# Moving five more stores of a mixture of softmaxes to ScalarE's DMA queue, with a new written order for the last ten units

## The chip, the cores and the metric

The kernel runs on one core of one Trainium2 chip. The metric is the device time of one execution, in microseconds (us), from the first instruction to the last. A profile of one execution lists every instruction and every DMA packet with its time; its span leaves out a little at both ends, so the execution's own time stands beside the span below.

## The reference

The input holds 32 batches of 128 rows, and in each row four heads with 4096 logits each. The output is one row of 4096 values: the four softmaxes, weighted with a softmax over the four prior values of that row.

```python
prior_probs = np.exp(prior - prior.max(axis=-1, keepdims=True))
prior_probs = prior_probs / prior_probs.sum(axis=-1, keepdims=True)
softmax = np.exp(logits - logits.max(axis=-1, keepdims=True))
softmax = softmax / softmax.sum(axis=-1, keepdims=True)
mixture = np.sum(prior_probs[..., None] * softmax, axis=2)   # logits: (32, 128, 4, 4096)
```

Everything is float32. The logits are 268.4 MB to be read, and the output is 67.1 MB to be written.

## The kernel before

**Tiles.** One batch is a *unit* (u = 0 to 31); its 128 rows lie on the 128 partitions. A head of a unit is a tile of 128x4096 floats, 2.1 MB. On-chip memory holds a ring of 12 such slots, thus three units. Head h of unit u goes to slot (4u + h) mod 12 (`place`, L101; the very last head is put one further), so unit u + 3 reuses the slots of unit u.

**Steps.** The kernel has no scheduler: the order is written out by hand as a string of words, and `run` (L193) turns each word into one call. A word names the step, then a head or the quarters of the 4096 columns it covers, then the unit (`@u`; in the repeated part `'` means the unit before and `+2` two units on). The quarters are 1024 columns wide: `34` is the last one, `03` the first three.

- L: load heads (L115, on SyncE's queue SP). `L03@u` brings heads 0 to 2 in one transfer of 6.3 MB, `L34@u` brings head 3.
- M: maximum of a head, negated (VectorE, L123). E: exponential with its sum (ScalarE, L128). R: reciprocal of the sum (VectorE, L134).
- G: a diagonal matrix of the head's weight (GpSimd, L137). X: the head times that diagonal, added up in the PSUM accumulator `acc` (TensorE, L146): `X123` is head 1, quarter 2 to 3. Heads 0 to 2 are summed in this way.
- C: the weight alone (GpSimd, L153). Z: head 3 (or a part of head 2) scaled in place (GpSimd, L157).
- A: head 3 weighted and added to the accumulator (VectorE, L163). For other quarters V copies the accumulator to head 1's slot (ScalarE, L182), and P adds it to the scaled head 3 (GpSimd, L185). W adds a scaled quarter of head 2 to head 3 (GpSimd, L179); for the quarters named in `BYPASS` head 2 is not sent through TensorE. B and T do the like on VectorE for the last unit.
- S: the store of a finished unit (L120). The result lies in head 3's slot, so `S@u` must have landed before `L34@u+3` may be issued.

**What sets the order.** Each engine works through its own instructions in the order of the words and waits by semaphore for its inputs. The two DMA queues (SP's and ScalarE's, q1 and q10 in the profile) each take transfers in the order in which their engine issued them; both are served by the same 16 DMA engines. A DMA instruction whose input isn't ready holds up everything behind it on its engine. Units 0 to 23 repeat one string (`STEADY`, L27): there, `S'` stands between two exponentials, and `L03+2 L34+2` follow. From unit 24 on, `ORDER` (L32 to L59) is a long string in which the steps of two units are mixed, matrix products are cut into quarters, and loads of units 29 to 31 are cut into heads. The queue of a store is chosen by its unit number in `store` (L118): ScalarE's for units 2 to 21, SP's for the others.

Of the kernel before, what the change touches and what calls it, by code (L numbers as in the profile page):

```python
# [26 lines left out]
STEADY = (  # L27
    "M0 E0 R3' C3' Z324' M1 R0 G0 A01' A12' V23' P23' V34' P34' E1 X0 S' L03+2 L34+2 "
    "M2 E2 R1 G1 X1 M3 E3 R2 G2 X2 "
)  # L30
ORDER = [STEADY] * 24
ORDER += [  # L32
    "M1@24 M0@24 E1@24 V23@23 M2@24 E0@24 R3@23 V34@23 R0@24 C3@23 G0@24 A01@23 Z324@23 "
    "X023@24 E2@24 R1@24 A12@23 X001@24 P23@23 M3@24 X012@24 P34@23 X034@24 R2@24 G1@24 "  # L34
    "E3@24 G2@24 X123@24 X112@24 M0@25 X101@24 S@23 X134@24 R3@24 E0@25 X212@24 M1@25 "
    "Z324@24 X234@24 C3@24 L03@26 X223@24 V34@24 A12@24 E1@25 P34@24 X201@24 R0@25 M3@25 "
    "G0@25 X012@25 V23@24 X034@25 P23@24 A01@24 E3@25 X023@25 M2@25 X001@25 R1@25 E2@25 "
    "R3@25 G1@25 C3@25 X134@25 Z324@25 L34@26 M0@26 X123@25 X101@25 S@24 X112@25 R2@25 "
    "E0@26 M1@26 G2@25 X201@25 X234@25 L03@27 X212@25 V34@25 R0@26 M3@26 G0@26 E1@26 "
    "P34@25 X223@25 X034@26 A12@25 V23@25 E3@26 P23@25 M2@26 X013@26 A01@25 E2@26 R1@26 "  # L40
    "X001@26 R3@26 G1@26 Z324@26 X101@26 L34@27 R2@26 G2@26 M0@27 C3@26 X123@26 X112@26 "
    "S@25 X134@26 M1@27 E0@27 X212@26 X234@26 L03@28 R0@27 X201@26 V34@26 M2@27 G0@27 "
    "E1@27 P34@26 X223@26 X034@27 A01@26 V23@26 M3@27 X001@27 E2@27 P23@26 X023@27 R1@27 "
    "E3@27 A12@26 G1@27 X123@27 R2@27 G2@27 Z234@27 X012@27 L34@28 R3@27 Z304@27 X112@27 "
    "M0@28 X212@27 X134@27 V12@27 C3@27 S@26 W34@27 M1@28 E0@28 X223@27 P12@27 X101@27 "
    "X201@27 L01@29 V34@27 R0@28 M2@28 G0@28 E1@28 P34@27 X034@28 X012@28 L12@29 V01@27 "
    "R1@28 M3@28 G1@28 X112@28 E2@28 P01@27 X001@28 X101@28 L23@29 M0@29 V23@27 E3@28 "
    "P23@27 X023@28 X134@28 R2@28 M1@29 Z224@28 L34@29 X123@28 E0@29 G2@28 X202@28 R3@28 "
    "V23@28 R0@29 C3@28 G0@29 S@27 A01@28 Z314@28 E1@29 M2@29 X001@29 X023@29 W23@28 "
    "V12@28 L01@30 V34@28 X012@29 R1@29 P12@28 M3@29 E2@29 X034@29 G1@29 W34@28 X101@29 "  # L50
    "L12@30 E3@29 R2@29 X112@29 P34@28 M0@30 X134@29 G2@29 P23@28 X201@29 V34@29 L23@30 "
    "R3@29 E0@30 M1@30 X123@29 Z304@29 X223@29 L34@30 V01@29 X212@29 C3@29 R0@30 V23@29 "
    "G0@30 M2@30 Z234@29 X001@30 E1@30 P01@29 X023@30 L01@31 W34@29 X034@30 V12@29 R1@30 "
    "M3@30 E2@30 X012@30 G1@30 P12@29 X112@30 L12@31 P34@29 X123@30 E3@30 M0@31 X134@30 "
    "P23@29 X101@30 L23@31 V34@30 R2@30 R3@30 G2@30 M1@31 E0@31 Z314@30 X223@30 X201@30 "
    "C3@30 L34@31 Z234@30 X212@30 V23@30 R0@31 A01@30 G0@31 E1@31 W34@30 X023@31 M2@31 "
    "X001@31 P34@30 S@28 V12@30 X034@31 P23@30 R1@31 E2@31 M3@31 X012@31 G1@31 P12@30 "
    "X134@31 S@29 X123@31 R2@31 E3@31 C2@31 G2@31 B234@31 X101@31 B223@31 S@30 X201@31 "
    "R3@31 C3@31 T23@31 X112@31 T34@31 X212@31 A01@31 S23@31 A12@31 S34@31 S01@31 S12@31 "  # L59
]  # L60

BYPASS = {
    (27, 3), (28, 2), (28, 3), (29, 3), (30, 3), (31, 2), (31, 3),
}


# [1 line left out]
def kernel(  # L68
# [6 lines left out]
    nc = tc.nc  # L75
# [31 lines left out]
    def home(u, a, b):  # L107
        return slot(u, 3, a, b)
# [7 lines left out]
            h += n  # L116

    def store(u, a=0, b=4):  # L118
        queue = nc.scalar if 2 <= u < 22 else nc.sync
        queue.dma_start(out=out[u, :, a * C : b * C], in_=home(u, a, b))  # L120

    def peak(u, h):
# [61 lines left out]
    def add_scaled(u, a, b):  # L184
        nc.gpsimd.tensor_add(home(u, a, b), slot(u, 1, a, b), slot(u, 3, a, b))  # L185

    step = {
        "L": load, "S": store, "M": peak, "E": exp, "R": recip, "G": diagonal, "X": weigh,
        "C": weight, "Z": scale, "A": add_last, "B": add_head, "T": add_both, "V": evac,
        "P": add_scaled, "W": add_second,  # L190
    }

    def run(u, words):  # L193
        for w in words.split():
            op, digits, back, on, at = re.fullmatch(
                r"([A-Z])(\d*)('*)(?:\+(\d+))?(?:@(\d+))?", w
            ).groups()
            v = int(at) if at else u - len(back) + int(on or 0)
            if 0 <= v < U:
                step[op](v, *map(int, digits))  # L200

    with tc.manual_schedule():
# [22 lines left out]

        for u, words in enumerate(ORDER):
            run(u, words)
# [30 lines left out]
```

## Time and profile before

| | |
|---|---|
| three runs | 787.1, 787.2, 787.32 us (median 787.2) |
| the profiled execution | 787.09 us, span 785.4 us |
| TensorE busy | 681.8 us, 87% of the span |
| VectorE busy | 645.1 us, 82% |
| ScalarE busy | 547.5 us, 70% |
| GpSimd busy | 293.8 us, 37% |
| DMA | 335.90 MB at a mean of 428 GB/s |
| packets of q1 (SP) and q10 (ScalarE) | 87.1% and 12.5% of 16 engines' span |

The row of DMA in the profile's picture of 40 slices says how busy the 16 DMA engines were; the rows of the engines say the same for each engine. A share of 100% for DMA means that packets lay end to end on all 16. In the list of waits, "SPq L115 <- DMA out_dram<-ring" is SP standing at a load until a store has landed. Such a wait is harmless as long as earlier transfers are still queued; how long they last is read from the time between the issue of a transfer and its first packet.

### The profile page before, as it was taken

How to read it: one execution, taken by the hardware profiler on the slowest of the kernel's cores; microseconds unless marked ns; L12 is line 12 of the kernel's file. 1: busy time of each engine (PE TensorE's matmuls, PEld its weight loads, DVE VectorE, ACT ScalarE, POOL GpSimd, SP SyncE). 2: the span in 40 equal slices, each digit the busy share in tenths (PEclk: the TensorE clock that was granted, in tenths of full speed). 3: DMA queues.
4: the chain of work that ended last, by engine and by line, in shares of the span. 5: the costliest groups of instructions: out<-in, count | busy, mean ns of one | idle time of the engine just before them, and what ended most of it. 6: DMA issues, size and time to landing. Idle time of an engine off the chain costs nothing.

```text
span 785.4 us, 4589 instructions
## 1 busy us (share of the span) xinstructions
PE 681.8 (87%) x1508; PEld 293.0 (37%) x1508; DVE 645.1 (82%) x327; ACT 547.5 (70%) x326; POOL 293.8 (37%) x243
## 2 busy tenths in 40 slices
PE   0959998989999888998989989898888998899996
PEld 0424433333344333433334334343333443344342
DVE  6489977897778977779877798777888887979895
ACT  2557867867668666686676776766857668779883
POOL 0033323433134332334322343323430544277892
PEclk9989999999989999999999989999989899999999
DMA  9999999999999999999999999999999999999998
GB/s 378 456 411 426 429 436 413 433 437 441 435 416 431 448 436 421 434 424 436 444 429 430 420 436 438 439 427 421 432 449 421 440 408 431 451 412 431 429 429 351
DMA packets 15335, 335.90 MB, mean 428 GB/s; under 512 B 1712, under 2 KB 1712, under 8 KB 2256
## 3 DMA queue, kind: packets, MB, share of 16 engines
q1 hardware_dynamic: 12384, 293.61, 87.1%
q10 hardware_dynamic: 2928, 42.01, 12.5%
q8 instruction: 12, 0.20, 0.1%
q14 instruction: 11, 0.09, 0.0%
HBM read 268.50 MB, written 67.11 MB: 427 GB/s over the span
## 4 chain that ended last, share of the span: by engine, by line
DMA 58%; DVE 12%; PE 10%; POOL 10%; ACT 5%; issue 4%; SPq 0%; POOLq 0%; ACTq 0%
DMA ring<-in_logits_dram 58%; DVE nmax L123 11%; PE acc L146 10%; POOL ring L185 7%; ACT ring L128 3%; ACT ring L182 2%; POOL ring L179 1%; POOL ring L157 1%; POOL diag L137 1%; DVE ring L163 0%; SPq L115 0%; DVE rden L134 0%; SPq L120 0%; POOLq L185 0%; POOLq L137 0%
## 5 line engine op out<-in xcount | busy, mean ns | idle before, releaser
L146 PE MATMUL acc<-ring,diag 128*128 128x512 f32 x1508 | 681.8, 613 | 96.6 <-ACT ring L182 62.0
L123 DVE TENSOR_REDUCE nmax<-ring 128x1 f32<-128x4096 f32 x128 | 563.0, 4409 | 114.6 <-DMA ring<-in_logits_dram 114.6
L128 ACT ACTIVATE ring<-ring,nmax 128x4096 f32<-128x4096 f32 x128 | 474.6, 3708 | 202.5 <-DVE nmax L123 202.1
L146 PEld LDWEIGHTS acc<-ring,diag 128*128 128x128 f32 x1508 | 293.0, 196 | 484.5 <-issue 358.2
L185 POOL TENSOR_TENSOR ring<-ring 128x1024 f32<-128x1024 f32 x68 | 160.1, 2374 | 20.1 <-ACT ring L182 11.2
L137 POOL TENSOR_SCALAR diag<-ident,rden,pp 128x128 f32<-128x128 f32 x96 | 43.0, 448 | 239.7 <-DVE rden L134 239.7
L153 POOL TENSOR_TENSOR wght<-rden,pp 128x1 f32<-128x1 f32 x33 | 6.3, 190 | 210.4 <-DVE rden L134 210.4
L182 ACT ACTIVATE ring<-acc 128x1024 f32<-128x1024 f32 x68 | 66.7, 1012 | 17.9 <-PE acc L146 13.8
L157 POOL TENSOR_SCALAR ring<-ring,rden,pp 128x2048 f32<-128x2048 f32 (+3 forms) x35 | 74.2, 2121 | 9.0 <-DVE rden L134 8.7
L163 DVE SCALAR_TENSOR_TENSOR ring<-ring,wght,acc 128x1024 f32<-128x1024 f32 x60 | 74.2, 1269 | 3.3 <-PE acc L146 2.3
L134 DVE RECIPROCAL rden<-dsum 128x1 f32<-128x1 f32 x128 | 19.3, 153 | 10.2 <-ACT ring L128 10.2
L128 ACT ACTIVATION_READ_ACCUMULATOR ring<-ring,nmax 128x1 f32 x128 | 24.2, 189 | 0.0
L179 POOL TENSOR_TENSOR ring<-ring 128x1024 f32<-128x1024 f32 x5 | 11.8, 2367 | 0.1
L213 DVE TENSOR_REDUCE pmax<-pr 32x128 f32<-32x512 f32 x1 | 0.7, 674 | 5.3 <-DMA pr<-in_prior_dram 5.3
L215 ACT ACTIVATE pr<-pr 32x512 f32<-32x512 f32 x1 | 0.6, 628 | 4.2 <-DVE pr L214 4.2
L163 DVE SCALAR_TENSOR_TENSOR ring<-ring,wght 128x1024 f32<-128x1024 f32 x2 | 2.5, 1280 | 0.3 <-POOL wght L153 0.3
L215 ACT ACT_TABLE_LOAD x1 | 1.3, 1283 | 1.2 <-PEq L242 1.2
L222 DVE STREAM_TRANSPOSE pp<-pn 32x128 f32<-32x128 f32 x4 | 1.2, 302 | 0.1
L216 DVE TENSOR_REDUCE pmax<-pr 32x128 f32<-32x512 f32 x1 | 0.7, 674 | 0.7 <-ACT pr L215 0.7
L218 DVE TENSOR_TENSOR pn<-pr,pmax 32x512 f32<-32x512 f32 x1 | 1.0, 1016 | 0.0
L217 DVE RECIPROCAL pmax<-pmax 32x128 f32<-32x128 f32 x1 | 0.9, 941 | 0.0
L214 DVE TENSOR_TENSOR pr<-pr,pmax 32x512 f32<-32x512 f32 x1 | 0.7, 680 | 0.0
(6 smaller groups left out, 0.9 us busy)
## 6 DMA issues: line engine op xcount, KB each, us to landing
ring<-in_logits_dram SPq DMA_DIRECT2D x27, 6144.0 KB, 34.3
ring<-in_logits_dram SPq DMA_DIRECT2D x43, 2048.0 KB, 25.5
out_dram<-ring ACTq DMA_DIRECT2D x20, 2048.0 KB, 16.1
out_dram<-ring SPq DMA_DIRECT2D x11, 2048.0 KB, 14.0
out_dram<-ring SPq DMA_DIRECT2D x4, 512.0 KB, 5.5
pr<-in_prior_dram ACTq DMA_DIRECT2D x1, 64.0 KB, 4.5
ring<-in_logits_dram SPq DMA_DIRECT2D x1, 39.5
```

The costliest lines, as they stand in the source:

```text
L123: nc.vector.tensor_reduce(out=nmax[:, u, h : h + 1], in_=slot(u, h), op=ALU.max, axis=AX.X, negate=True)
L128: nc.scalar.activation(slot(u, h), slot(u, h), AF.Exp, bias=nmax[:, u, h : h + 1], accum_out=dsum[:, u, h : h + 1],)
L134: nc.vector.reciprocal(rden[:, u, h : h + 1], dsum[:, u, h : h + 1])
L137: nc.gpsimd.tensor_scalar(out=diag[:, u % 2, h], in0=ident, scalar1=rden[:, u, h : h + 1], scalar2=pp[:, h, u : u + 1], op0=ALU.mult, op1= ...
L146: nc.tensor.matmul(acc[:, k * W : (k + 1) * W], lhsT=diag[:, u % 2, h], rhs=e[:, k * W : (k + 1) * W], start=h == 0, stop=h == H - 2 or (u ...
L153: nc.gpsimd.tensor_mul(wght[:, u, h : h + 1], rden[:, u, h : h + 1], pp[:, h, u : u + 1])
L157: nc.gpsimd.tensor_scalar(out=e, in0=e, scalar1=rden[:, u, h : h + 1], scalar2=pp[:, h, u : u + 1], op0=ALU.mult, op1=ALU.mult,)
L163: nc.vector.scalar_tensor_tensor(out=o, in0=slot(u, h, a, b), scalar=wght[:, u, h : h + 1], in1=more, op0=ALU.mult, op1=ALU.add,)
L179: nc.gpsimd.tensor_add(e, e, slot(u, 2, a, b))
L182: nc.scalar.activation(slot(u, 1, a, b), acc[:, a * C : b * C], AF.Copy)
L185: nc.gpsimd.tensor_add(home(u, a, b), slot(u, 1, a, b), slot(u, 3, a, b))
L215: nc.scalar.activation(pr, pr, AF.Exp)
```

## The change

The stores of units 22 to 26 are issued by ScalarE instead of SP. The repeated string ends two units earlier (22 copies instead of 24), and the written order from unit 22 on is a new one. The set of quarters that bypass TensorE changes from seven to eight: units 27, 28 (2), 29, 30 and 31 (2) become units 25, 28, 29 (2), 30 (2) and 31 (2). All other functions stay the same. The diff, cut to the lines of the new order from the store of unit 24 on, and to the same places of the old one:

```diff
-ORDER = [STEADY] * 24
+ORDER = [STEADY] * 22
 ORDER += [
...
-    "P23@27 X023@28 X134@28 R2@28 M1@29 Z224@28 L34@29 X123@28 E0@29 G2@28 X202@28 R3@28 "
-    "V23@28 R0@29 C3@28 G0@29 S@27 A01@28 Z314@28 E1@29 M2@29 X001@29 X023@29 W23@28 "
-    "V12@28 L01@30 V34@28 X012@29 R1@29 P12@28 M3@29 E2@29 X034@29 G1@29 W34@28 X101@29 "
...
-    "P23@29 X101@30 L23@31 V34@30 R2@30 R3@30 G2@30 M1@31 E0@31 Z314@30 X223@30 X201@30 "
-    "C3@30 L34@31 Z234@30 X212@30 V23@30 R0@31 A01@30 G0@31 E1@31 W34@30 X023@31 M2@31 "
-    "X001@31 P34@30 S@28 V12@30 X034@31 P23@30 R1@31 E2@31 M3@31 X012@31 G1@31 P12@30 "
-    "X134@31 S@29 X123@31 R2@31 E3@31 C2@31 G2@31 B234@31 X101@31 B223@31 S@30 X201@31 "
-    "R3@31 C3@31 T23@31 X112@31 T34@31 X212@31 A01@31 S23@31 A12@31 S34@31 S01@31 S12@31 "
...
+    "G1@25 X101@25 L03@27 S@24 M0@26 E2@25 X112@25 X034@25 X134@25 R2@25 E0@26 R3@25 "
+    "G2@25 M1@26 Z234@25 X123@25 C3@25 Z324@25 X201@25 V34@25 W34@25 X223@25 R0@26 E1@26 "
+    "M2@26 X212@25 G0@26 P34@25 X034@26 V23@25 L34@27 A12@25 E2@26 P23@25 X023@26 R1@26 "
+    "M3@26 X012@26 G1@26 X123@26 L03@28 X112@26 R2@26 E3@26 M0@27 G2@26 X212@26 X134@26 "
+    "V12@26 A01@25 E0@27 X223@26 R3@26 M1@27 C3@26 Z314@26 X001@26 X101@26 V23@26 P12@26 "
+    "S@25 X234@26 R0@27 E1@27 M3@27 G0@27 X201@26 P23@26 X012@27 V34@26 A01@26 X023@27 "
+    "E3@27 P34@26 R1@27 M2@27 X001@27 G1@27 X123@27 S@26 X112@27 R3@27 E2@27 M0@28 C3@27 "
+    "Z304@27 X034@27 L34@28 X134@27 R2@27 E0@28 M1@28 G2@27 X101@27 L01@29 X213@27 V12@27 "
...
+    "L34@29 X123@28 R2@28 M1@29 G2@28 E0@29 Z234@28 X201@28 X223@28 L01@30 V34@27 R3@28 "
+    "X212@28 R0@29 Z324@28 M2@29 V23@28 X034@28 E1@29 P34@27 X134@28 C3@28 G0@29 A01@28 "
+    "P23@28 X023@29 V34@28 S@27 M3@29 E2@29 X001@29 W34@28 X034@29 P34@28 A12@28 E3@29 "
+    "L12@30 R1@29 X012@29 R2@29 M0@30 G1@29 Z224@29 X101@29 G2@29 X201@29 L23@30 R3@29 "
...
+    "G2@30 Z224@30 X112@30 L23@31 X123@30 V34@30 R3@30 E0@31 Z314@30 X101@30 M1@31 "
+    "X212@30 L34@31 W34@30 X201@30 V12@30 R0@31 V23@30 M2@31 G0@31 P12@30 X034@31 E1@31 "
+    "S@29 X012@31 W23@30 X023@31 E2@31 R1@31 M3@31 G1@31 C3@30 X134@31 P34@30 S@28 "
+    "X123@31 P23@30 A01@30 E3@31 X112@31 R2@31 C2@31 X001@31 G2@31 B223@31 S@30 B234@31 "
+    "X101@31 R3@31 C3@31 T34@31 X201@31 T23@31 X212@31 A01@31 S34@31 A12@31 S23@31 S01@31 "
+    "S12@31 "
 ]
 BYPASS = {
-    (27, 3), (28, 2), (28, 3), (29, 3), (30, 3), (31, 2), (31, 3),
+    (25, 3), (28, 3), (29, 2), (29, 3), (30, 2), (30, 3), (31, 2), (31, 3),
 }
 
     def store(u, a=0, b=4):
-        queue = nc.scalar if 2 <= u < 22 else nc.sync
+        queue = nc.scalar if 2 <= u < 27 else nc.sync
         queue.dma_start(out=out[u, :, a * C : b * C], in_=home(u, a, b))
```

In each engine's own order, the new one differs from the old at these places. On ScalarE the stores stand like this: `E2@23 S@22 E3@23`, `E3@24 S@23 E2@24`, `E3@25 S@24 E2@25`, then `E0@27 V23@26 S@25 E1@27 V34@26 E3@27 S@26 E2@27`. On SP no store stands among the loads of units 25 to 29; `S@27` comes behind `L01@30` and ahead of `L12@30`, and `S@29` ahead of `S@28`. On GpSimd `P34@27` comes behind `Z234@28` and `Z324@28`. On TensorE one quarter of one head is four instructions in the profile, and one quarter more bypasses it, so there are 1504 of them instead of 1508.

## The prediction

> **What bounds the kernel now.** I read the head of the page first (span, DMA row), then the windows by stage, then the DMA issues and SP's waits, and last the chain of waits at the end.
>
> ```profile
> DMA  9999999999999999999999999999999999999998
> q1 hardware_dynamic: 12384, 293.61, 87.1%
> q10 hardware_dynamic: 2928, 42.01, 12.5%
> out_dram<-ring ACTq DMA_DIRECT2D x20, 2048.0 KB, 16.1
> out_dram<-ring SPq DMA_DIRECT2D x11, 2048.0 KB, 14.0
> ```
>
> The DMA engines are busy in every slice, and the two queues' packets together fill 99.6% of 16 engines' span. A store lands 16.1 us after its issue on ScalarE's queue and 14.0 us after on SP's. By stages (columns: window, busy time and instructions of each engine, TensorE's clock, DMA share, GB/s):
>
> ```profile
> 97.00:582.00 485.00, 431.32 (x958) 185.87 (x956) 398.11 (x199) 338.39 (x200) 163.28 (x141) 0.96 1.00 432
> 582.00:703.00 121.00, 110.97 (x241) 47.52 (x242) 102.29 (x51) 87.14 (x52) 50.38 (x39) 0.94 1.00 428
> 703.00:776.00 73.00, 69.71 (x159) 29.37 (x159) 66.75 (x35) 64.96 (x42) 57.35 (x39) 1.00 1.01 429
> 776.00:785.30 9.30, 2.36 (x6) 0.76 (x4) 2.75 (x3) 0.00 (x0) 0.00 (x0) 0.89 0.67 273
> ```
>
> With stores on ScalarE's queue (97 to 582) the share is 1.00 at 432 GB/s; with stores on SP's (582 to 703) it is 1.00 at 428. Only the last 9 us fall off. So DMA bounds the time up to about 776 us, and the end of the compute chain bounds the rest. In the stage that is changed, SP does wait, mostly for stores to land:
>
> ```profile
> SPq L115 <- DMA out_dram<-ring: 78.0, 6, 17.1
> SPq L120 <- DVE ring L163: 53.1, 10, 9.8
> SPq L120 <- POOL ring L185: 39.3, 5, 17.9
> ```
>
> The reader should see that these waits, from 580 us on, cost nothing yet: the share in the same window is 1.00. How near they come is in the trace's packet records, put to transfers in the order of their queue: in the stage from 586 us a transfer's first packet comes 3.3 us (the store issued at 617.10) to 19.9 us after its issue, mostly 6 to 12 us. That is the backlog which covers a wait. At the end:
>
> ```profile
> 755.08 3.38 DVE nmax L123
> 758.46 0.91 ACT ring L182
> ...
> 767.79 10.58 PE acc L146 x24
> 778.37 0.03 issue
> 778.39 1.28 DVE ring L163
> ```
>
> The chain runs over the maximum of the last unit's head 1, GpSimd, and TensorE's last 24 products to the last addition; the last store follows it.
>
> **The change part by part.** The sum is made against the profiled execution: 787.09 us, its span 785.4 and 1.7 around it. The median of the runs is 787.2, 0.1 above. What a measurement can tell from no change I take as 0.2%, 1.57 us.
>
> *Bytes and issue time.* Nothing is added to the 335.90 MB. Five issues move from SP (0.34 us each in the rows of its timeline) to ScalarE (0.36). That is 1.8 us on an engine that is 70% busy, beside exponentials; in the repeated stage twenty of these lie there at a DMA share of 1.00. Cost 0. If DMA were not the cover, an exponential would come 0.36 us later.
>
> *The store's wait on ScalarE.* Behind it stands one exponential. With T for the landing of a unit's three-head load (M starts 0.99 us later: 133.46 to 134.45), maxima of 4.41 and exponentials of 3.7, `S@22` to `S@24` come behind an exponential that ends 18 to 21 us after T. Their last inputs P take two or three GpSimd steps (2.05 + 2.37 + 2.37) after a reciprocal at T + 10, so T + 17. No stall; 0. SP in turn runs ahead: `L03@26` to `L03@28` go out at about T + 17 with some 11 us queued.
>
> *The slower rate of 582 to 703.* By the windows it is worth 121 us x (1 - 428/432) = 1.1 us at most. By the packets it is less: the 16 KB packets of the stage take 611 to 614 ns in most transfers, 621 and 651 in two, and all that they lie above 611 (and the 48 KB ones above 1815) sums to 0.6 us, in a patch at 622 to 645 us that no store order explains. Ends 0 and -1.1; I take -0.3, near the packets.
>
> *`L34@28`, the thin place.* `S@25` stands on ScalarE behind `E0@27`: T27 + 0.99 + 4.43 + 3.9, and V's 0.9, thus issued at T27 + 10.3. In before it went at 662.98, that is T27 - 3.9 (T27 was 666.90), and the load that needs its slot at 677.02, with 11.0 us still queued. Now the store's first packet comes 3.4 us after issue (100.14 to 103.50 in the repeated stage), at T27 + 13.7. Beside the three-head load, each engine takes a 48 KB packet and a 16 KB one in turn: the repeated stage's store took 103.50 to 115.31 for eight packets per engine, which alone need 8 x 0.611 = 4.9 us. So `L34@27`, `L03@28` and `S@25` (4.9 + 14.5 + 4.9) are through together at T27 + 24.3, with the store the last. `L34@28` goes out 1.0 us after (115.31 to 116.29) and starts 0.9 to 2.0 us after that (the issues at 775.15 and 770.09 found a short queue). On SP's queue nothing else may pass it, so 1.9 to 3.0 us stand open. What fills them is `S@26`, queued behind `S@25`: M0, one addition of 1.27, M1 and M3 end at T27 + 15.8, `E3@27` at T27 + 19.6; issued at 19.8, first packet at 23.2, covered till 29.2. It is 1.1 us in time. Ends 0 and +3.0; I take 0, because each step has a row, and the cover is 2 to 3 us long.
>
> The Trainium skill says otherwise of sharing: in "DMA: Bandwidth & Descriptors", "Queues, rings and completion order", each engine takes turns between queues by whole packets of some 9 to 17 descriptors. By that, a store's eight pieces would go in one turn, `S@25` would be through at about T27 + 19, an estimate, and the place would not be thin at all. The 11.8 us of the trace's stores speak against it, and the sum keeps to them.
>
> *`S@27` and the loads behind it.* The store is issued by SP and holds up `L12@30`, `L23@30`, `L34@30`. Its input `P34@27` now stands behind `Z324@28`, which needs a reciprocal that VectorE gave at 717.7 in before. 717.9 + 2.05 + 2.37 and issue make 722.4, perhaps 2 us less since `L03@28` lands earlier. In before it went at 712.36 with 5.9 us queued. The queue now holds `L01@30` ahead of it, to 718.84 + 4.9 = 723.7; with 0.9 to 2.0 us to the first packet, 0 to 0.7 us stand open. I take +0.2. GpSimd is the one behind; `Z224@29` and later steps have slack, for its steps from `G1@29` to `W34@30` sum to some 27 us of 40.
>
> *The end.* `G0@31` waits for GpSimd:
>
> ```profile
> 755.29 2.91 POOL L157 TENSOR_SCALAR ring<-ring,rden,pp 128x3072 f32<-128x3072 f32 x1
> 758.18 0.18 POOL L153 TENSOR_TENSOR wght<-rden,pp 128x1 f32<-128x1 f32 x1
> 758.35 1.19 POOL L157 TENSOR_SCALAR ring<-ring,rden,pp 128x1024 f32<-128x1024 f32 x1
> 759.74 0.45 POOL L137 TENSOR_SCALAR diag<-ident,rden,pp 128x128 f32<-128x128 f32 x1 [0.21 <-DVE rden L134]
> ```
>
> Ahead of it there is now `Z314@30`, free to start at 754.8, and `W34@30`: 754.8 + 2.91 + 2.37 = 760.1, against 759.74. Both orders have ten quarters (40 products) behind it, 18.2 us in before, so TensorE ends 0.4 us later, and with it the last addition and the last store. `S@30` goes at about 770.9 (before 770.09), as the stores ahead of it end at 772.6: 0.3 us open, but not on the last store's path. The quarter more that bypasses TensorE (4 products of about 0.44) lies earlier. Cost +0.4. Ends: -0.9 (what of the 2 us of idle DMA before 783.96 a better order could get) and +0.9.
>
> Sum: 0 + 0 - 0.3 + 0 + 0.2 + 0.4 = +0.3. On the median: 787.2 + 0.3 = 787.5.
>
> **The rivals.**
>
> *Slower: the cover of `L34@28` fails.* If `S@26` is issued after T27 + 20.9, DMA runs dry. All later loads wait for `L34@28` and go out that much later. Its price is at most 3.0 us, typically 2.4: 787.5 + 2.4 = 789.9. For it: the backlog falls from 11.0 us to none on q1, and the margin is one short step of ScalarE. Against it: ScalarE is idle 30%. From 1.3 us of dry time on (0.3 are there already) it decides the sign.
>
> *Slower: `P34@27` is later than reckoned.* One more GpSimd step of 2.37 us ahead of it, or `V34@27` late behind `E0@29`, opens 0.7 to 2.4 us at `S@27`: up to 789.6, typically 788.6. For it: a step moved back by 10 us (712.36 to 722.4). Against: VectorE's row is dense there, and its order the same.
>
> *Faster: the loads gain.* SP is freed of five waits, the slow patch goes (-0.6 to -1.1), and the end gains up to 0.9: 787.2 - 0.6 - 0.6 = 786.0 typically, 785.2 with all. For it: 432 against 428 GB/s. Against: the share is 1.00 on both sides, so there is no gap to close; faster needs both gains nearly whole.
>
> The Trainium skill speaks against this gain: "DMA: Bandwidth & Descriptors", "Issuing engines are not separate DMA queues", says that DMAs of both queues run on the same 16 engines, and several issuers save only issue time. The trace agrees in the packets, 611 and 1815 ns in either stage.
>
> That the change doesn't do what it says can't be: q10 must rise by five stores of 2.1 MB.
>
> **How the numbers follow.** Forecast (786.8 to 788.4 on its own): 0.61. The cover fails: 0.15. `P34@27` late: 0.10, half of it over the bound. Gain: 0.14, of which 0.06 lies below 785.6. Slower by over 0.2% is 0.15 + 0.05 and 0.01 of the forecast's own spread, 0.21; faster 0.06; same 0.73. The range goes from 786.2 (half of the gain cut off) to 789.7 (most of the cover's case within, with its longest gaps cut off).
>
> **What would show it.** In the changed profile: q10 at about 15.6% (12.5 + 5 x 0.6), q1 at 84; SP's waits for a store's landing without a dip in GB/s. The window of 24 us after T28 shows the cover: a share of 1.00 says it holds; 0.9 or less in 2 us says that it fails. `S@25` issues 10 us after T27, `S@26` 9.5 us after that; `S@27` near 721 to 722. The share at 722 to 726 shows the second rival. At the end, `G0@31` near 760.1 and the last addition near 778.7. The prediction is wrong if a load is issued later than its queue lasts at a place I have not walked (units 22 to 24), or if TensorE's clock, 0.86 to 1.00 by window, slows the new order of products.

## The result, and the profile after

The changed kernel takes 788.46 us (median of 18 executions), the kernel before 787.09 us beside it (18 executions). The ratio of the means is 1.0022 (of the medians 1.0017), with a 95% interval of 1.0015 to 1.0029: slower by about 0.2%. A second session gave 789.65 against 787.39, ratio 1.0026 (1.0017 to 1.0035). More telling than the median is the scatter: executions of the kernel before lie between 786.52 and 787.80 us, those of the changed one between 786.86 and 791.18. The profile that came with the result is of the shortest one, 786.86 us (span 785.1), which is even 0.2 us shorter than the profiled execution of before.

The page of that execution, DMA row, queues and stores (the line numbers of the changed kernel are 7 higher: its loads are L122, its products L153, its copies L189):

```profile
DMA  9999999999999999999999999999999999999998
q1 hardware_dynamic: 11664, 283.12, 84.0%
q10 hardware_dynamic: 3648, 52.50, 15.6%
out_dram<-ring ACTq DMA_DIRECT2D x25, 2048.0 KB, 16.1
out_dram<-ring SPq DMA_DIRECT2D x6, 2048.0 KB, 12.7
```

Its windows by stage (the columns as before: window, busy time of each engine, clock, DMA share, GB/s) and SP's waits from 580 us on:

```profile
97.00:582.00 485.00, 432.45 (x957) 185.91 (x956) 399.52 (x200) 339.01 (x200) 163.23 (x140) 0.96 1.00 432
582.00:703.00 121.00, 107.60 (x243) 45.30 (x242) 101.38 (x50) 88.80 (x55) 51.90 (x39) 0.99 1.00 429
703.00:776.00 73.00, 69.73 (x160) 29.53 (x159) 67.98 (x38) 62.49 (x39) 56.11 (x38) 1.00 1.01 429
```

```profile
SPq L122 <- DMA out_dram<-ring: 92.9, 6, 31.3
```

The five stores moved, and this execution is no slower for it. But SP's longest wait for a store to land grew from 17.1 to 31.3 us. That is the wait of `L34@28` for `S@25`, and it ends with nothing queued: the load goes out at 691.09, its first packet comes 0.97 us later, at 692.06.

So the question is what a longer execution does. One of 790.07 us is among the runs below, with every word of the program the same. Three windows of the short one and then of the long one; the clock is the third number from the end:

```profile
625.00:640.00 15.00, 15.00 (x36) 6.59 (x35) 14.66 (x8) 12.39 (x9) 7.76 (x6) 1.00 1.01 432
657.00:666.00 9.00, 9.00 (x21) 4.09 (x22) 5.08 (x4) 7.49 (x5) 3.25 (x3) 1.00 0.98 421
666.00:688.00 22.00, 18.82 (x44) 8.01 (x43) 20.04 (x10) 15.29 (x10) 12.11 (x9) 1.00 1.00 431
```

```profile
625.00:640.00 15.00, 14.27 (x27) 6.16 (x28) 13.73 (x9) 11.43 (x7) 7.16 (x6) 0.80 1.01 433
657.00:666.00 9.00, 9.00 (x22) 3.99 (x21) 4.89 (x4) 7.25 (x4) 3.10 (x3) 1.00 0.84 343
666.00:688.00 22.00, 18.90 (x38) 7.92 (x37) 19.37 (x9) 14.25 (x9) 11.00 (x7) 0.84 1.00 415
```

From 625 to 640 us the granted clock of TensorE was 0.80 instead of 1.00; from 657 to 666, 17 us later, DMA moved 343 GB/s instead of 421. (In windows as short as these the share itself is off by up to 0.06, since packets that cross an edge are counted on one side; therefore idle DMA is given below from the packets, as the time in which fewer than 16 lay open, each missing one counted as a sixteenth.) The chain of waits of the long execution joins the two:

```profile
625.23 0.46 POOL diag L144
625.69 0.04 issue
625.73 11.45 PE acc L153 x20
637.18 0.02 issue
637.20 0.04 ACT ring L189
...
640.71 23.12 DMA out_dram<-ring
...
664.36 27.63 DMA ring<-in_logits_dram
```

The reader should see a chain that the chain of before never had: TensorE's products of unit 24, ScalarE's copy of them (L189), a store (`S@24`, issued at 640.71 after GpSimd's addition), 23 us until it has landed, and only then the loads behind. In the short execution the second copy of unit 24 starts at 633.58 and `S@24` goes out at 637.94; in the long one at 637.20 and 640.71, 2.77 us later. Not all of that is the clock: 1.04 us were there already at the first maximum of unit 25, which waits for `L03@25` to land and starts at 619.53 in the short and at 620.57 in the long execution.

```profile
633.58 1.02 ACT L189 ACTIVATE ring<-acc 128x1024 f32<-128x1024 f32 x1 [0.50 <-PE acc L153]
```

```profile
637.20 1.02 ACT L189 ACTIVATE ring<-acc 128x1024 f32<-128x1024 f32 x1 [2.35 <-PE acc L153]
```

### The profile page after: what moved, and what is told of

Read it like the earlier page. It is cut to its first block, busy times and chain, and to the rows that moved or that the text cites. A ratio compares the mean times of both kernels' runs of the same rounds, so it can differ in the third digit from the quotient of the medians.

```text
span 785.1 us, 4581 instructions
## 1 busy us (share of the span) xinstructions
PE 679.1 (86%) x1504; PEld 290.8 (37%) x1504; DVE 646.2 (82%) x328; ACT 547.0 (70%) x325; POOL 293.7 (37%) x243
## 3 DMA queue, kind: packets, MB, share of 16 engines
q10 hardware_dynamic: 3648, 52.50, 15.6%
## 4 chain that ended last, share of the span: by engine, by line
DMA 60%; PE 10%; DVE 9%; POOL 9%; ACT 6%; issue 5%; SPq 0%; POOLq 0%; ACTq 0%; DVEq 0%
DMA ring<-in_logits_dram 59%; PE acc L153 10%; DVE nmax L130 9%; POOL ring L192 7%; ACT ring L135 4%; ACT ring L189 2%; DMA out_dram<-ring 1%; POOL ring L164 1%; POOL diag L144 0%; SPq L122 0%; POOL ring L186 0%; DVE ring L170 0%; DVE rden L141 0%; POOL wght L160 0%; POOLq L192 0%
## 5 line engine op out<-in xcount | busy, mean ns | idle before, releaser
L153 PE MATMUL acc<-ring,diag 128*128 128x512 f32 x1504 | 679.1, 612 | 98.4 <-ACT ring L189 56.1
L153 PEld LDWEIGHTS acc<-ring,diag 128*128 128x128 f32 x1504 | 290.8, 196 | 486.0 <-issue 350.2
L189 ACT ACTIVATE ring<-acc 128x1024 f32<-128x1024 f32 x67 | 65.5, 1010 | 9.8 <-PE acc L153 9.6
```

The lines of the kernel that those rows point to most:

```text
L153: nc.tensor.matmul(acc[:, k * W : (k + 1) * W], lhsT=diag[:, u % 2, h], rhs=e[:, k * W : (k + 1) * W], start=h == 0, stop=h == H - 2 or (u ...
L189: nc.scalar.activation(slot(u, 1, a, b), acc[:, a * C : b * C], AF.Copy)
```

## The experiments

Theory A says that the loss lies where a load may only go out when a store has landed, and the store lands late because on its own queue it shares the engines with the loads. Rival B puts it at unit 27's store on SP; rival C says that two queues cost time everywhere.

**The changed kernel again, and two single executions of it.** No edit.

> The changed kernel itself. Theory A: the loss comes from one place, the load of unit 28's head 3, which may go out only when unit 25's store has landed and is covered by unit 26's store alone; the cover's timing differs from run to run. Then this gives again a median near 788.4 us with single runs between 786.9 and 791, and the profile has its only low DMA share between 688 and 696 us. Rival B: the loss lies at unit 27's store, which SP issues behind one load of unit 30 with next to no queue left; then the low share is at 722 to 728 us. Rival C: two queues cost time wherever loads and stores share the engines late in the run; then the share is 1.00 everywhere and packets are longer than 611 and 1815 ns.

> The changed kernel once more, one execution, to see where a longer one loses. Theory A: an execution of 789.5 us or more shows idle DMA at the load of unit 28's head 3 (688 to 696 us) or at unit 27's head 3 (657 to 668 us), each of which waits for a store drawn out by sharing. Theory D: no idle DMA, but packets longer than 611 and 1815 ns. An execution below 788 shows neither.

> The same kernel and the same question as the look before it.

Measured: 789.65 us (787.91 to 791.07) in the first; its profile is of 788.54 us. The single executions took 787.88 and 790.07 us. All traces of programs that are the same up to `S@24` can be put in one table, nine of them with the kernels below. All but the clock and TensorE's idle time is from the packet and issue records; "lost" is the idle time of DMA plus what packets took above 0.611 us (16 KB) and 1.815 us (48 KB), over 16 engines.

| execution, us | TensorE idle before unit 24's last products, us | clock 625 to 640 us | `S@24` issued | landed | queue left at `L34@27`, us | lost from 655 to 686, us |
|---|---|---|---|---|---|---|
| 786.86, changed | 1.84 | 1.00 | 637.94 | 655.38 | 4.92 | 0.07 |
| 787.88, changed | 3.54 | 1.00 | 638.65 | 656.46 | 3.93 | 0.08 |
| 789.31, `s26_late` | 3.57 | 1.00 | 638.76 | 657.53 | 2.67 | 0.08 |
| 788.62, `p34_early` | 3.54 | 1.00 | 638.90 | 657.36 | 3.05 | 0.08 |
| 788.54, changed | 1.89 | 1.00 | 638.96 | 657.34 | 2.71 | 0.08 |
| 787.63, `both_early` | 3.59 | 0.89 | 639.53 | 659.47 | 0.98 | 0.66 |
| 791.92, `s25_early` | 4.73 | 0.89 | 640.35 | 662.65 | 0.97 | 1.89 |
| 790.07, changed | 4.73 | 0.80 | 640.71 | 663.19 | 0.96 | 2.02 |
| 793.17, `s26_gone` | 4.73 | 0.78 | 641.07 | 663.81 | 0.96 | 2.40 |

"Landed" is the last packet; "queue left" is the time from the load's issue to its first packet, and about 1 us is what an empty queue takes. The five executions with a clock of 1.00 lose nothing at this place. The four with a lower clock issue the store 1.6 to 3.1 us later than the first, find the queue empty and lose 0.7 to 2.4 us. That delay has two parts. In the five the store goes out 18.4 us after the first maximum of unit 25 starts, in the four 19.2 to 20.4 us after it: the slower products make 0.8 to 2.0 us. The rest, 0.7 to 1.6 us, is that the maximum itself starts later than in the first, because `L03@25` lands later; in the five it does so by up to 1.0 us, without a loss. Why it lands later is open. One us of delay at the issue makes 2.7 us at the landing, for the later the store starts, the more of its packets stand beside 48 KB ones.

The clock in its turn goes with TensorE's idle time just before these products, while it waits for GpSimd's diagonal of unit 24's head 2: 1.8 to 3.6 us in the five executions, 3.6 to 4.7 us in the four others. The short execution and the one of 790.07 us:

```profile
624.70 20.87 PE L153 MATMUL acc<-ring,diag 128*128 128x512 f32 x48 [1.84 <-POOL diag L144]
```

```profile
625.73 19.58 PE L153 MATMUL acc<-ring,diag 128*128 128x512 f32 x39 [4.73 <-POOL diag L144]
```

That the idle time brings the lower clock is suggested by this, not shown: 3.57 and 3.59 us stand on different sides, and no run changed the idle time alone.

The second place is `L34@28`: from 686 to 702 us the three changed executions with a clock of 1.00 lose 0.38, 0.57 and 0.94 us, in the order of their times; before loses 0.07 us from 687 to 700. Of the 1.7 us that 788.54 has over 786.86, 0.6 are this place; the rest is spread over smaller amounts and the end. Of the 790.07, 2.0 us are `L34@27` and 0.66 `L34@28`. At 718 to 732 us (rival B) none of the changed ones shows idle DMA, and packets elsewhere have their usual lengths (rival C, or theory D).

**Unit 25's store earlier, unit 27's input earlier, and both.** Three kernels, each moving words only. The edits, with the removed words at their old places:

```diff
 # s25_early
-    "... V12@26 A01@25 E0@27 ... V23@26 P12@26 S@25 ..."
+    "... A12@25 A01@25 E2@26 ... E3@26 S@25 M0@27 ..."
 # p34_early
-    "... E0@29 ... L01@30 V34@27 R3@28 ... E1@29 P34@27 ..."
+    "... V34@27 E3@28 P34@27 ..."
 # both_early: both
```

> The last addition of unit 25 is moved up to stand behind the one before it, and unit 25's store to stand behind the fourth exponential of unit 26, some 8 us earlier. Theory A: the load of unit 28's head 3 goes out with 6 us or more still queued, median 786.9 us (786.5 to 787.3), no run over 788.2. Rival B: the median stays near 788.4 with single runs to 791. Rival C: the same as B.

> The copy and the GpSimd addition that unit 27's store waits for are moved ahead by some 10 us, to stand around the last exponential of unit 28. Theory A: no change, median near 788.4 us, single runs to 791. Rival B: median 787.0, no run over 788.2. Rival C: near 788.4.

> Both moves at once. Theory A: as with unit 25's store alone, 786.9 us. Rival B: as with the GpSimd addition alone, 787.0. If both places cost, only this one reaches 786.6 to 787.0 and each move alone stays above it by 0.3 us or more. Rival C: 788.4 whatever is moved.

Measured: 790.84 us (789.27 to 791.92), 789.94 (788.62 to 790.48) and 788.12 (787.03 to 789.33); ratios 1.0045, 1.0033 and 1.0010 (1.0001 to 1.0019). So neither move alone helps. For `p34_early` theory A had said so, and rival B is not the whole loss; `s25_early` fell plainly short of its expectation. Together the moves bring the loss from 2.3 us, the changed kernel's in the same session, to 0.7, still 1.1 us more than expected. The trace of `s25_early` says why it gains nothing alone. `L34@28` does find 7.4 us queued now. But with `S@25` early among the loads, `L03@28` lands at 692.80 instead of the short execution's 688.71, and VectorE's work on unit 28, and with it `P34@27` and `S@27`, comes 4.6 us later (725.37). Part of this is what was lost at `L34@27`: the 790.07 us execution, which lost as much there, has 691.01 and 722.89, and no idle time behind. In `s25_early` DMA idles for 1.58 us from 718 to 732 us, the place of rival B:

```profile
718.00:732.00 14.00, 14.00 (x34) 6.12 (x33) 13.71 (x7) 12.20 (x8) 11.24 (x8) 1.00 0.90 357
```

A gain at one place was paid back at the next: in the changed kernel the late `S@25` is what lets `L03@28` land early enough for `S@27`. The 791.92 us of this trace also hold 1.9 us at `L34@27`, which neither move touches.

**The cover taken away.** Unit 26's store was first moved behind one more exponential (`s26_late`, behind `E2@27`), then behind two (`s26_gone`, behind `E0@28`).

```diff
-    "... E3@27 P34@26 R1@27 M2@27 X001@27 G1@27 X123@27 S@26 X112@27 R3@27 E2@27 M0@28 ..."
+    "... X123@27 X112@27 R3@27 E2@27 S@26 M0@28 ..."              # s26_late
+    "... X123@27 X112@27 R3@27 E2@27 M0@28 ... E0@28 S@26 M1@28 ..."  # s26_gone
```

> The changed kernel with unit 26's store moved behind one more exponential on ScalarE, so that nothing covers the gap between unit 25's store and the load of unit 28's head 3. Theory A: DMA idles 2 to 3 us between 688 and 696 us in the profile, and the median rises by 1.5 to 2.5 us over the changed kernel's, to 790.5 or more. Rivals B and C: no change, near 789.

> The changed kernel with unit 26's store two exponentials later on ScalarE, behind the first of unit 28, which can't start before unit 28's load has landed. Nothing is left to cover the wait for unit 25's store. Theory A: DMA idles some 2 us from about 689 us on, and the median is 1.5 to 2.5 us over the changed kernel's, 790 to 791. If the cover is worth nothing, the median stays at the changed kernel's 788.5 to 789.7.

Measured: `s26_late` 790.04 us (788.91 to 790.87), not told apart from the changed kernel's 789.65 of the other session, and without the idle time that was expected (0.41 us). ScalarE issued the store at 687.59 instead of 684.02 only, 1.9 us before `S@25`'s last packet (689.47), and its first packet followed within 1.3 us (688.89), in time. That test was too weak. `s26_gone` is not: 793.07 us (791.93 to 794.01), ratio 1.0067, 3.4 to 4.6 us above the changed kernel's two medians and 2 us more than expected. Two of its windows:

```profile
657.00:666.00 9.00, 9.00 (x22) 3.99 (x21) 5.25 (x4) 7.39 (x4) 3.24 (x3) 1.00 0.87 350
...
688.00:696.00 8.00, 7.29 (x17) 2.88 (x16) 4.76 (x3) 3.48 (x3) 3.51 (x2) 1.00 0.64 240
```

From 687 to 700 us DMA idles 2.21 us, and packets take 1.60 us more than usual after it. So `S@26` does cover the wait of `L34@28`, and its absence costs more than the gap itself. The 350 GB/s in the first line are the same execution's loss at `L34@27`, with a clock of 0.78.

**Queue and order apart.** `queue_alone` is the order of before with all five stores on ScalarE's queue, `queue_22` has unit 22's alone there; `order_alone` is the new order with all five on SP's.

```diff
 # queue_alone, in the kernel before      # queue_22: 2 <= u < 23
-        queue = nc.scalar if 2 <= u < 22 else nc.sync
+        queue = nc.scalar if 2 <= u < 27 else nc.sync
 # order_alone, in the changed kernel
-        queue = nc.scalar if 2 <= u < 27 else nc.sync
+        queue = nc.scalar if 2 <= u < 22 else nc.sync
```

> The order of before, with the stores of units 22 to 26 on ScalarE's queue: the queue part of the change alone. Theory A (the new order leaves too little time between the landing of a store and the load that needs its slot; the queue itself costs nothing): 786.9 to 787.6 us, at most 0.3 above before, single runs within 1.5 us of each other. Rival C (two queues cost time by sharing): 788.2 or more with single runs to 790.

> The order of before with unit 22's store alone on ScalarE's queue, which is where the repeated string has its stores. Theory A: the queue costs nothing where the store is issued as early as in the repeated string, 787.1 to 787.6 us with single runs within 1 us of each other. Rival C: a part of what all five stores cost in the order of before (1.0 us), thus 787.6 to 787.9 with more spread.

> The new order, with the stores of units 22 to 26 on SP's queue again. On one queue a store is not drawn out by the loads behind it, and unit 26's store stands ready behind unit 25's. Theory A with the shared queues as the cause of the late landings: 786.9 to 787.6 us and little spread. Theory A with the order alone as the cause: the load of unit 28's head 3 still waits for unit 25's store, 788.2 us or more. Rival C: as before, 787.2, for no store shares.

Measured: `queue_22` 787.38 us (787.05 to 788.01) against 787.54, ratio 0.9998 (0.9989 to 1.0007). Where the store is issued as early as in the repeated string, no cost of the queue is seen, and no gain. `queue_alone` 788.57 us (787.37 to 789.54), ratio 1.0013 (1.0004 to 1.0022): the queue part alone does cost, more than theory A had allowed. In its trace `S@23` and `L03@26` go out together at 616.72 with 2.1 us queued, the store lands at 639.36 (before: 628.04), and `L34@26` finds 3.4 us (before: 10.5). From 636 to 646 us this execution loses 1.0 us (before: 0.3). That is the same mechanism at another store, in an order that was not made for it. The trace is of one of the two shortest executions (787.45), so where the longer ones lose is not shown. Rival C's version, a cost everywhere, has no support in `queue_22`, though the interval there reaches to 0.6 us above before and so does not exclude the 787.6 to 787.9 us that C gave it. More weighs `three_places` below: all five stores are on ScalarE's queue there, and no loss is seen.

`order_alone` 794.80 us (794.44 to 795.21), ratio 1.0093 (1.0080 to 1.0107). The sign is that of the order as the cause, but the size and the place are not those I named. I had thought of `S@25` and not of `S@24`: on SP's queue it stands behind `L03@27`, lands at 670.13, and `L34@27` waits for it with nothing else queued: 4.6 us are lost there.

```profile
657.00:675.00 18.00, 17.56 (x41) 7.46 (x41) 16.62 (x9) 15.35 (x11) 8.80 (x7) 1.00 0.76 308
```

There is a second place that I had not named: on SP's queue `S@22` stands ahead of `L34@24` and holds it back to 592.47 (changed kernel: 578.38), and 2.2 us are lost from 586 to 606 us. So the new order is 5 to 6 us worse without the second queue, and the sum of the parts is not the whole: queue +1.0, order +7.2, both +1.4 in one session (788.46 - 787.09) and +2.3 in the other (789.65 - 787.39).

**All three places.** `both_early`, and one word more: VectorE's reciprocal of unit 24's head 2 stands ahead of the first maximum of unit 25 instead of behind it.

```diff
-    "... E2@24 M0@25 G1@24 ... X101@24 R2@24 E0@25 ..."
+    "... E2@24 R2@24 M0@25 G1@24 ... X101@24 E0@25 ..."
```

> Both moves at once (unit 25's store and the GpSimd addition that unit 27's store waits for), and the reciprocal of unit 24's third head ahead of the first maximum of unit 25, where VectorE stands idle. TensorE then gets unit 24's last products some 5 us earlier, and unit 24's store no longer waits for them when the granted clock is low. Theory A, with three thin places (the loads of unit 27's and 28's head 3 and unit 27's store) as the whole of the loss: 787.2 to 787.9 us, no run over 788.6, and the load of unit 27's head 3 finds 2 us or more still queued. If the loss is elsewhere: as both moves without it, 788.1, with runs to 789.3.

In the changed kernel that reciprocal waits at 623.87 behind a maximum, though the exponential it needs ended at 618.83, and VectorE stood idle until 619.53 for the load:

```profile
619.53 4.42 DVE L130 TENSOR_REDUCE nmax<-ring 128x1 f32<-128x4096 f32 x1 [4.47 <-DMA ring<-in_logits_dram]
623.87 0.15 DVE L141 RECIPROCAL rden<-dsum 128x1 f32<-128x1 f32 x1
```

Measured: 787.40 us (786.76 to 788.46) against 787.33, ratio 0.9999 (0.9990 to 1.0008). With the three places mended no loss is left that can be seen, and the scatter is that of before (in the same session: 786.76 to 788.25). The changed kernel was not run in that session, and the interval overlaps that of `both_early`, so the worth of the one word more is less sure than that of all three moves. In its trace DMA is idle for 0.07 us between 560 and 762 us; `L34@27`, `L34@28` and `S@27` find 4.6, 3.4 and 6.9 us queued. The moved word does not make `S@24` earlier while the clock is 1.00 (it goes out at 638.44, again 18.4 us after the first maximum of unit 25); what it takes away is TensorE's wait ahead of unit 24's last products, which now follow the earlier ones at once. No execution with a lower clock was traced of this kernel. At the end DMA idles 1.25 us ahead of unit 30's store, issued at 772.22 instead of 770.21, and the last addition comes at 779.81 instead of 777.57; why is open. It is not faster than before; no version that was tried is.

## Why the prediction came out as it did

The median lies within the range (786.2 to 789.7), 1.0 us above the forecast of 787.5. It is at the border of the forecast's case (786.8 to 788.4), and the second session's 789.65 lies beyond it. Some executions cost what the forecast said, others what the rival with the chance of 0.15 said (789.9), but not for the rival's reason: the 790.07 us execution lost 2.0 us at `L34@27`, which no rival names, and 0.66 at `L34@28`, the rival's place. That the median lies in the range is in part luck: the sum left out the place that costs most, and its term for the end had the wrong sign in the short execution. I had looked for one time where there is a spread of times.

- *Bytes, issue time.* Right. q10 went to 15.6% and q1 to 84.0% as reckoned.
- *The store's wait on ScalarE, 0.* The stall didn't come, but the sentence "SP in turn runs ahead" is the step that failed. It spoke of the loads `L03`, which do go out with 8 to 13 us queued in the short execution, and passed over `L34@27`, which must wait for `S@24`'s landing. That landing was not reckoned at all. The only transfer time that the sum has for a store is the repeated stage's 11.8 us, and it was misread as one beside the three-head load: in the trace of before that store's neighbours are 123 packets of 16 KB and 24 of 48 KB. `S@24` took 14.1 us in the short execution (91 and 55) and 19.0 in the long one (22 and 120). And the issue hangs on TensorE's last products when the granted clock is low, which I had named at the end, as units 22 to 24 and as the clock, without walking it. This term was 0 and measured 0.07 us in the short execution and 2.0 in the long one.
- *The slower rate of 582 to 703, -0.3.* Right: 429 against 428 GB/s, and the packets of 600 to 657 us lose 0.15 us where before lost 0.56.
- *`L34@28`, 0 of 0 to 3.0.* The place, the store it waits for and its cover were right, and the instant nearly so: first packet at T27 + 25.8 (T27 = 666.28), forecast 26.2 to 27.3. The size 0 was wrong: 0.4 to 0.9 us, and not more for two reasons that offset each other. `S@25` and `S@26` were issued at T27 + 6.2 and 17.7 instead of 10.3 and 19.8, since ScalarE issues a store while the exponential ahead of it still runs, but the load came 2.15 us after the store's last packet, not 1.0. The price without cover, 3.0 at most, was too low: `s26_gone` paid 3.8.
- *`S@27`, +0.2.* Issued at 720.73 (forecast 722.4, perhaps 2 us less), 0.01 us idle. The rival's place is real, as `s25_early` showed, but not in the changed kernel itself.
- *The end, +0.4.* Wrong in sign for the short execution. The order on GpSimd is as told:

```profile
754.28 2.91 POOL ring L164
757.19 0.07 issue
757.26 1.84 POOL ring L186
...
759.60 0.46 POOL diag L144
760.06 0.04 issue
760.10 17.45 PE acc L153 x40
777.55 0.02 issue
777.57 1.28 DVE ring L170
```

  `G0@31` runs at 759.60 (forecast 760.1), since `Z314@30` started 0.5 us earlier, and the 40 products need 17.45 us, not 18.2, as they run in one piece, where in before the last 24 waited for GpSimd (from 767.79). The last addition comes at 777.57, 0.8 us earlier than before. So the short execution ends 0.2 us ahead of before, although it lost 0.4 us at `L34@28`.
- *The rival "gain"* was right not to be the forecast: the share was 1.00 on both sides. The Trainium skill's sentence that several issuers save only issue time ("DMA: Bandwidth & Descriptors", "Issuing engines are not separate DMA queues") agrees with `queue_22`'s 0.9998. The other rule of the Trainium skill that was weighed (same page, "Queues, rings and completion order"), turns by packets of 9 to 17 descriptors, does not hold in these traces: `S@24` of the 790.07 us execution took 19.0 us beside 48 KB packets, and eight turns of 0.611 + 1.815 are 19.4.

What is shown: the landing of the store is what `L34@27` waits for, a late issue of `S@24` leaves that load without a queue, and the three moves together take the loss and the scatter away. What is not: the lower clock goes with the late `S@24` in all nine traces, but a late `L03@25` has a part in it, no run held the clock fixed, and that TensorE's idle time causes it is argued.

## What to carry to other kernels

A transfer moved to a second queue no longer delays the loads behind it, but it lands later itself, and later still beside larger packets: from first packet to last `S@24` took 7.1 us on SP's queue in before, and 14.1 to 19.0 us on ScalarE's in the changed kernel. Look for who waits for the landing. Where DMA is busy all the time, read from the issue of each transfer to its first packet how much is still queued, at every load and not only at the thinnest one; here a load with 2.7 to 4.9 us left in five executions had none in four others, and the median of a kernel with such places is a mixture. Mending one of several such places may only move the loss to the next one.

## What the runs showed that was not expected

- ScalarE issues a store while an earlier exponential still runs: `S@25` at 672.49, inside one of 671.25 to 674.96, although a copy stands between the two.
- After DMA ran empty, packets took longer than usual for a while: 1.60 us over 16 engines in `s26_gone`, beside 2.21 us of idle time.
- The clock granted to TensorE between 625 and 640 us was 1.00, 0.89, 0.80 or 0.78 in nine executions of nearly the same program, and the load behind `S@24` found its queue empty in just those with less than 1.00. The lower clock comes in stretches: in the long execution it was 0.51 from 624.1 to 631.0 us, in the short one 0.50 from 616.7 to 620.0, where it did no harm. The profile of the kernel before has 0.86 from 582 to 630 us, where its loads found 7 to 13 us queued, and no idle DMA there.
